# Down projection of a two-layer hybrid backbone: half-precision pairs with one scale a layer in nine of eleven block pairs, and conditioning products 1024 wide

## The chip, the core and the metric

The kernel runs on one core of a Trainium2 chip, as one program in one launch. The metric is the device time of an execution in microseconds (us); the time of a kernel is the median of its runs.

## What is computed

Two transformer-like layers over 1024 latent tokens and 256 context tokens of width 1024. The mixers (Fourier and Hyena in layer 0, neighbourhood attention in layer 1) are not touched. Each layer ends with a gated feed-forward block whose inner width is 2816, scaled and shifted by columns that come from a conditioning vector:

```
def ada_mod(cond, w, b):
    m = (jax.nn.silu(cond) @ w + b)[..., None, :]
    return jnp.split(m, 6, axis=-1)

def swiglu(u, w_gate, w_up, w_down):
    return (jax.nn.silu(u @ w_gate) * (u @ w_up)) @ w_down
...
        h_lat = h_lat + g2 * swiglu(modulate(rms_norm(h_lat, norm2_g[i]), sh2, sc2),
                                    ffn_w_gate[i], ffn_w_up[i], ffn_w_down[i])
```

Everything is float32 in and out. The kernel reaches that precision by splitting an operand x into a high part and the rest, `hi` and `lo`, and adding three products: hi*hi, hi*lo, lo*hi.

## The kernel before, in words

Tokens lie along the free dimension, channels on the 128 partitions. The inner width of 2816 is 22 blocks of 128, taken as 11 pairs of blocks (`n2 = 11`).

**Gate and up** (`ffn`, L1374; one iteration i a pair). Each of gate and up is one Winograd form of a 2x2 block product: seven products in place of eight, each of 12 matmuls (four blocks of the contraction, three hi/lo combinations) of 128x512. `wino_steps` (L1324) gives the matmuls; ScalarE copies partial sums out of PSUM (`snap`, L1329), VectorE adds others (L1338, L1348, L1353). TensorE alternates between the two chains, so that a copy has about one product of the other chain to finish in. Weights and activations here are half-precision (f16) pairs: `half_split` (L1146 on ScalarE, L1147 on VectorE) multiplies by a scale, writes the f16 `hi`, and then `lo`. The scale comes from a bound for each weight tile: `weight_scale` sums absolute values on ScalarE (L1183, with the accumulator) and sums these over the partitions with a matmul.

`finish(i)` multiplies up by the silu of gate (L1422), forms the four hidden blocks' Winograd combinations (L1425 to L1428) and writes seven of them to DRAM (`bops`) on POOL's queue (L274). `sums(i)` does the same for four weight blocks of down (loads on SP's queue, L268; L1388 to L1391; `sops` in DRAM). Layer 0 calls `sums` once an iteration, layer 1 twice in iterations 1 to 5.

**Down** (`down`, L1493). Again a Winograd form over the whole layer: seven products p, each summed over the 11 pairs i, with 12 matmuls a pair (L1511). `operands` loads a weight block and a hidden block, 512 columns each, into one 128x1024 tile, and `split` (L287 on ScalarE, L289 on VectorE) writes fp32r `hi` and `lo` tiles; in four of the seven products the loaded tile is also the `lo` tile. At the end of a product VectorE evicts four PSUM banks into the residual (`evict`, L1532), scaled by a conditioning column. Two sets of four banks alternate. In layer 0 the conditioning products of layer 1 run beside gate, up and Down: `ada_group` multiplies a 128x1024 weight tile by the broadcast conditioning vector and sums along the row, in two halves of 512 (L448) that a third operation adds (L450).

**What sets the order.** The order of instructions on each engine is made at build time, by a scheduler that runs down the program text; each engine then works through its own list. Tiles come from pools in rotation: a tile is free when the last use of the one that had its place is over. The pool `p4` has 20 buffers of 128x1024 float32 (`S4`); Down's operands and the conditioning weights come from it. `T()` takes small tiles from a pool of six and, two times of eight, from another.

## Time and profile before

| | us |
|---|---|
| median of 3 runs (3014.61 to 3021.31) | 3015.26 |
| the profiled execution | 3016.71 |
| its span, first to last instruction | 3014.9 |
| TensorE (PE) busy | 2864.5 |
| VectorE (DVE) busy | 2108.4 |
| ScalarE (ACT) busy | 1511.8 |
| first and last matmul of Down, both layers | 1359.5 and 2996.7 |

Each group row names line, engine, operation, tiles written and read, shapes and count; behind the bar stand the busy time of the group in us (of overlapping instructions only once), the mean duration of one in ns, and the engine's idle time just ahead of them with what ended it. PEld is TensorE's weight load, which runs beside the matmuls. A row of a stretch gives the busy time of each engine in it, with the number of instructions that lie in it wholly or partly, the granted clock, the share of time that the DMA engines were busy, and GB/s. A row of waits gives who waited for whom: total us, times, longest. In a timeline row the time in brackets is the idle time ahead of the instruction and what ended it.

### The profile page before, as it was taken

The numbers are of one execution on the slowest core, as the hardware profiler recorded it, in microseconds if no ns is written. First come the engines' busy times: TensorE is split into PE (matmuls) and PEld (weight loads), VectorE is DVE, ScalarE is ACT, GpSimd is POOL, SyncE is SP. The second block draws the span as 40 slices with busy tenths as digits, with TensorE's granted clock in tenths as the row PEclk, the third lists the DMA queues.
The fourth block names the chain that finished last, engine by engine and source line by source line (L and its number), as shares of the span: only waits on it lengthen the run. The fifth ranks groups of instructions, "written<-read, shape, count | busy, mean of one in ns | idle before, by whom it ended". The sixth has DMA issues, their size and how long they took to land. (4 is left out here: it accounts for less than half of the span.)

```text
span 3014.9 us, 46087 instructions
## 1 busy us (share of the span) xinstructions
PE 2864.5 (95%) x16364; PEld 2085.2 (69%) x16364; DVE 2108.4 (70%) x4181; ACT 1511.8 (50%) x2761; POOL 530.8 (18%) x883
## 2 busy tenths in 40 slices
PE   7899999899998999999999999999999799999997
PEld 3678888888897444447778888878777344444886
DVE  5767786674677988866767437777776898765555
ACT  4663325452456555443445336777774655543433
POOL 1012013451111212131020002222231022112000
PEclk9899999999999999999999999999999899999999
DMA  7564545366555555657874344444555376424663
GB/s 256 190 202 166 176 143 173 119 189 213 200 210 196 211 187 206 221 207 270 290 245 153 126 130 119 134 137 121 180 175 192 134 275 235 149 81 165 217 192 130
DMA packets 253681, 551.47 MB, mean 183 GB/s; under 512 B 33926, under 2 KB 69448, under 8 KB 253450
## 3 DMA queue, kind: packets, MB, share of 16 engines
q1 hardware_dynamic: 191658, 357.63, 35.7%
q0 software_dynamic: 59488, 186.70, 17.5%
q10 hardware_dynamic: 2304, 4.20, 0.4%
q8 instruction: 129, 2.11, 0.3%
q14 instruction: 102, 0.84, 0.1%
HBM read 420.20 MB, written 119.80 MB: 179 GB/s over the span
## 5 line engine op out<-in xcount | busy, mean ns | idle before, releaser
L1324 PE MATMUL ps<-s,s 128*128 128x512 f16 x2100 | 477.3, 383 | 16.5 <-DVE s L1221 8.6
L1324 PEld LDWEIGHTS <-s 128*128 128x128 f16 x2640 | 259.1, 98 | 334.5 <-issue 28.4
L283 PE MATMUL ps<-s,wh 128*128 128x256 f32 (+1 forms) x1780 | 393.6, 327 | 1.5 <-ACT wh L287 1.5
L283 PEld LDWEIGHTS ps<-s,wh 128*128 128x128 f32 x1780 | 293.2, 188 | 36.5 <-ACT wh L287 3.1
L283 PE MATMUL pq<-s,wh 128*128 128x512 f32 (+1 forms) x972 | 297.4, 385 | 4.7 <-DVE s L2088 2.5
L1511 PE MATMUL ps<-s,s 128*128 128x512 f32 (+1 forms) x1000 | 261.2, 384 | 9.0 <-DVE s L289 8.7
L287 ACT CAST s<-s 128x1024 fp32r<-128x1024 f32 (+2 forms) x188 | 171.7, 942 | 180.0 <-DMA s<-d 146.9
L283 PE MATMUL ps<-s,wl 128*128 128x256 f32 (+1 forms) x890 | 257.7, 327 | 2.3 <-DVE wl L289 2.3
L283 PE MATMUL ps<-s,s 128*128 128x64 f16 (+3 forms) x2663 | 216.1, 233 | 24.0 <-DVE st L1800 9.9
L287 ACT CAST wh<-ws 128x1024 fp32r<-128x1024 f32 (+1 forms) x99 | 100.4, 1014 | 265.5 <-PE ps L283 163.8
L289 DVE TENSOR_TENSOR s<-s,s 128x1024 fp32r<-128x1024 f32 (+2 forms) x166 | 190.8, 1182 | 45.7 <-ACT s L287 44.8
L1511 PEld LDWEIGHTS ps<-s,s 128*128 128x128 f32 x1000 | 183.8, 188 | 50.3 <-DVE s L289 14.1
L289 DVE TENSOR_TENSOR wl<-ws,wh 128x1024 fp32r<-128x1024 f32 (+1 forms) x99 | 116.6, 1178 | 128.3 <-ACT wh L287 123.7
L283 PEld LDWEIGHTS pq<-s,wh 128*128 128x128 f32 x972 | 176.3, 191 | 39.4 <-DVE s L2088 2.7
L1324 PE MATMUL ps<-s,wh 128*128 128x512 f16 x624 | 190.9, 386 | 3.1 <-ACT wh L1146 2.1
L283 PE MATMUL ps<-s,mat 128*128 128x512 f32 x684 | 177.2, 405 | 6.8 <-DVE s L289 4.0
L283 PE MATMUL pq<-s,wl 128*128 128x512 f32 (+1 forms) x486 | 180.8, 381 | 0.1
L335 ACT CAST mat<-cs 128x1024 fp32r<-128x1024 f16 (+2 forms) x120 | 111.7, 935 | 132.1 <-PE ps L283 38.0
L283 PEld LDWEIGHTS ps<-s,wl 128*128 128x128 f32 x890 | 163.2, 188 | 20.3 <-DVE wl L289 3.7
L274 POOL DMA_DIRECT2D d<-s x153 | 82.7, 541 | 521.3 <-DVE s L1388 224.3
L283 PEld LDWEIGHTS ps<-s,mat 128*128 128x128 f32 x684 | 130.6, 194 | 42.0 <-DVE s L289 6.8
L1511 PE MATMUL ps<-s 128*128 128x512 f32 (+1 forms) x500 | 152.4, 387 | 1.1 <-ACT s L287 1.0
(393 smaller groups left out, 5825.4 us busy)
## 6 DMA issues: line engine op xcount, KB each, us to landing
s<-d SPq DMA_DIRECT2D x286, 256.0 KB, 3.7
s<-in_down SPq DMA_DIRECT2D x154, 256.0 KB, 4.6
d<-s POOLq DMA_DIRECT2D x137, 256.0 KB, 2.5
d<-tk POOLq DMA_DIRECT2D x98, 256.0 KB, 3.3
s<-in_ada_w POOLq DMA_DIRECT2D x48, 512.0 KB, 4.4
g<-in_bias POOLq DMA_DIRECT2D x128, 192.0 KB, 3.2
s<-in_up SPq DMA_DIRECT2D x46, 512.0 KB, 3.5
s<-in_gate SPq DMA_DIRECT2D x44, 512.0 KB, 4.1
```

The lines of the kernel that those rows point to most:

```text
L274: self.last_ldr = self.nc.gpsimd.dma_start(out, in_).ins
L283: self.nc.tensor.matmul(o, l, r, start=st, stop=sp)
L287: self.last_hi = nc.scalar.copy(hi, src).ins
L289: self.last_lo = eng.tensor_tensor(lo, src, hi.bitcast(F32), SUB).ins
L335: self.nc.scalar.copy(m, st)
L1324: nc.tensor.matmul(ps, x[:, sl], y, start=first and j == 0 and x is wh and y is xh, stop=j == 3 and x is wl, skip_group_check=True)
L1511: m = nc.tensor.matmul(acc[j][:, c0:c1], x[:, sl], y[:, xs], start=first and k == 0, stop=last and k == 2, skip_group_check=True)
```

## The change

Down's operands become f16 pairs in the pairs i = 0 to 8 of each product; pairs 9 and 10 stay fp32r, with both scales multiplied into their weight half. For that, one scale for the weights and one for the hidden blocks is made a layer: absolute sums of each pair's four weight blocks (in `sums`) and four hidden blocks (in `finish`) go to the columns of one tile, `sums_of`; one reduction, one matmul of 18 columns and a few operations on columns (`down_scales`, called in the last iteration of gate and up) give both scales, and the eviction's column takes their inverse. The loaded tile is now always one of its own, and both halves of a pair lie in one tile. The conditioning products of layer 1 are one operation of 1024 elements each. The diff, without its smallest pieces:

```
-    def weight_scale(self, tiles):
...
+    def abs_sums(self, tiles, st):
+
         junk = self.T(BF16, 1024)
         for k, t in enumerate(tiles):
-            nc.scalar.activation(junk[:, :t.shape[1]], t, AF.Abs, scale=2.0 ** -15, accum_out=st[:, k:k + 1])
+            self.nc.scalar.activation(junk[:, :t.shape[1]], t, AF.Abs, scale=2.0 ** -15, accum_out=st[:, k:k + 1])
+
+    def over_partitions(self, sums):
+
+        st = self.pt.tile([P, 16], F32, tag="st", name=self.nm("st"))
+        n = sums.shape[1]
+        sb = st.bitcast(BF16)[:, :n]
+        with self.nc.allow_low_precision(reason="a bound, within a factor of two"):
+            self.nc.vector.tensor_reduce(sb, sums, axis=AX, op=ADD)
         ps = self.PS()
-        self.mm(ps[:, 0:1], self.ones.bitcast(BF16)[:, 1::2], sb[:, 0:1], True, True)
+        self.mm(ps[:, :n], self.ones.bitcast(BF16)[:, 1::2], sb, True, True)
+        return ps[:, :n]
...
             for c in reversed(conds):
+                col = self.ada[(l, c)][:, nb:nb + 1]
+                if where != "s2":
+                    o = t if c == 0 else self.T(BF16, 1024)
+                    nc.vector.tensor_tensor_reduce(o, t, self.condw[c], 1.0, 0.0, MUL, ADD, col)
+                    continue
...
+            if i < nh:
+                self.abs_sums(t, sums_of[:, 4 * i:4 * i + 4])
             nc.vector.tensor_tensor(a22, a21, a22, ADD)
...
                 nc.vector.scalar_tensor_tensor(g, up[k], inv, g, op0=MUL, op1=MUL)
+            if i < nh:
+                self.abs_sums(list(gate.values()), sums_of[:, 4 * (nh + i):4 * (nh + i) + 4])
...
             up.to(1)
+            if i == n2 - 1:
+                scales = self.down_scales(l, nh)
...
+    def down_scales(self, l, n):
+
+        nc = self.nc
+        dc = self.C(8)
+        big, sw, sh, both, inv = dc[:, 0:2], dc[:, 2:3], dc[:, 3:4], dc[:, 4:5], dc[:, 5:6]
+        bounds = self.over_partitions(self.sums_of.rearrange("p (i k) -> p i k", k=4))
+        nc.vector.tensor_reduce(big[:, 0:1], bounds[:, :n], axis=AX, op=MAX)
+        nc.vector.tensor_reduce(big[:, 1:2], bounds[:, n:], axis=AX, op=MAX)
+        nc.vector.tensor_scalar(big, big, 1e-30, None, op0=MAX)
+        nc.vector.reciprocal(dc[:, 2:4], big)
+        nc.vector.tensor_tensor(both, sw, sh, MUL)
+        nc.vector.tensor_tensor(inv, big[:, 0:1], big[:, 1:2], MUL)
+        gcol = self.C(8)
+        nc.vector.tensor_scalar(gcol, self.ada[(l, 0)][:, 40:48], inv, None, op0=MUL)
+        return sw, sh, both, gcol
...
-        def operands(asrc, bsrc, own):
-            hi, lo = self.S4(F32R), self.S4(F32R)
-            f = self.S4() if own else lo.bitcast(F32)
+        def operands(asrc, bsrc, last):
+            f = self.S4()
             self.ld(f[:, :512], asrc)
             self.ld(f[:, 512:], bsrc)
-            self.split(f, hi, lo)
+            fa, fb = f[:, :512], f[:, 512:]
+            if last:
+                hi, lo = self.S4(F32R), self.S4(F32R)
+                nc.scalar.activation(hi[:, :512], fa, AF.Copy, scale=both)
+                nc.scalar.copy(hi[:, 512:], fb)
+                nc.vector.scalar_tensor_tensor(lo[:, :512], fa, both, hi[:, :512].bitcast(F32), op0=MUL, op1=SUB)
+                nc.vector.tensor_tensor(lo[:, 512:], fb, hi[:, 512:].bitcast(F32), SUB)
+            else:
+                t = self.S4(F16, 2048)
+                hi, lo = t[:, :1024], t[:, 1024:]
+                self.half_split(fa, sw, hi[:, :512], lo[:, :512])
+                self.half_split(fb, sh, hi[:, 512:], lo[:, 512:])
             return hi, lo
...
-            nc.vector.scalar_tensor_tensor(t, acc[j][:, c0:c0 + n], self.ada_col(l, pc, 5, nb), t, op0=MUL, op1=ADD)
+            nc.vector.scalar_tensor_tensor(t, acc[j][:, c0:c0 + n], gcol[:, nb:nb + 1], t, op0=MUL, op1=ADD)
...
-                ops = operands(src, bops[i][bk], ak in raw)
+                ops = operands(src, bops[i][bk], i >= n2 - 2)
```

Lines move: in the change L1153 and L1154 are `half_split`, L1187 the absolute sums, L1347 the copies out of PSUM, L1356 an addition to one, L1444 the multiplication in `finish`, L1501 and L1503 the silu, L1585 the eviction in Down, L450 the conditioning product, L1342 the matmuls of gate and up and L1564 those of Down.

ScalarE's list in layer 0, around the start of the fourth pair's up product, reads as follows in before (`g` are gate's hidden blocks and `tk` those of up, `ps` PSUM banks, `ws` and `s4` the next weights):

```order
L1475 ACTIVATE g_2686_10968<-g_2686_10968,c_5_93 128x512
L1146 ACTIVATE wh_2768_11460<-ws_2738_11249,c_5_93 128x1024
L1329 COPY g_2726_11180<-ps_2725_11167 128x512
L1475 ACTIVATE g_2726_11180<-g_2726_11180,c_5_93 128x512
L1329 COPY tk_2748_11332<-ps_2747_11319 128x512
L1183 ACTIVATE t_2800_11588,st_2799_11587<-ws_2797_11583 128x1024
L1183 ACTIVATE t_2800_11588,st_2799_11587<-s4_2798_11584 128x1024
L1329 COPY g_2745_11302<-ps_2725_11167 128x512
```

The same place in the change:

```order
L1153 ACTIVATE wh_2762_11449<-ws_2736_11246,c_5_93 128x1024
L1501 ACTIVATE g_2687_10968<-g_2687_10968,c_5_93 128x512
L1187 ACTIVATE t_2724_11203,c_7_94<-g_2687_10968 128x512
L1187 ACTIVATE t_2724_11203,c_7_94<-g_2688_10982 128x512
L1347 COPY tk_2747_11330<-ps_2746_11317 128x512
L1187 ACTIVATE t_2724_11203,c_7_94<-g_2691_11028 128x512
L1347 COPY g_2723_11172<-ps_2722_11159 128x512
L1501 ACTIVATE g_2723_11172<-g_2723_11172,c_5_93 128x512
L1187 ACTIVATE t_2781_11535,c_7_94<-g_2723_11172 128x512
```

Four sums (L1187) have come between the silu and the copies; the first of them reads a block that VectorE's multiplication (L1444) writes after the silu just ahead of it.

VectorE's list in Down of layer 0, at the end of the second product, in before (`s4` are operands, L1532 the four evictions of that product, L474 sums of squares):

```order
L289 TENSOR_TENSOR s4_3266_14299<-s4_3267_14300,s4_3265_14298 128x1024
L448 ISA s4_3263_14292,ah_3264_14294<-s4_3263_14292,s4_2525_10140 128x512
L448 ISA ah_3264_14294 128x1
L1532 SCALAR_TENSOR_TENSOR s2_3190_13935<-ps_3162_13798,c_13_100,s2_3190_13935 128x512
L1532 SCALAR_TENSOR_TENSOR s2_3191_13937<-ps_3163_13799,c_13_100,s2_3191_13937 128x512
L450 TENSOR_TENSOR c_17_102<-ah_3264_14294 128x1
L1532 SCALAR_TENSOR_TENSOR s2_3192_13939<-pq_3164_13800,c_13_100,s2_3192_13939 128x512
L1532 SCALAR_TENSOR_TENSOR s2_3193_13941<-pq_3165_13801,c_13_100,s2_3193_13941 128x512
L289 TENSOR_TENSOR s4_3273_14337<-s4_3273_14337,s4_3272_14336 128x1024
```

The same place in the change:

```order
L1154 SCALAR_TENSOR_TENSOR s4_3256_14481<-s4_3255_14478,c_3139_13645,s4_3256_14481 128x512 x2
L1154 SCALAR_TENSOR_TENSOR s4_3259_14504<-s4_3258_14501,c_3139_13645,s4_3259_14504 128x512 x2
L1585 SCALAR_TENSOR_TENSOR s2_3175_13928<-ps_3156_13794,c_3143_13656,s2_3175_13928 128x512
L450 ISA s4_3257_14498,c_19_103<-s4_3257_14498,s4_2527_10141 128x1024
L450 ISA c_19_103 128x1
L1585 SCALAR_TENSOR_TENSOR s2_3176_13930<-ps_3157_13795,c_3143_13656,s2_3176_13930 128x512
L1585 SCALAR_TENSOR_TENSOR s2_3177_13932<-pq_3158_13796,c_3143_13656,s2_3177_13932 128x512
L1585 SCALAR_TENSOR_TENSOR s2_3178_13934<-pq_3159_13797,c_3143_13656,s2_3178_13934 128x512
L1550 SCALAR_TENSOR_TENSOR s4_3262_14525<-s4_3260_14521,c_3139_13645,s4_3261_14524 128x512
```

Counted from the start of Down, 22 pairs are split ahead of this eviction in before, which is all of the two products, and 31 in the change, nine pairs into the third. At the ends of the first and the third to sixth products the counts are 14, 33, 44, 55 and 66 in before (the products hold 11, 33, 44, 55 and 66 pairs), and 19, 41.5, 53, 65 and 74 in the change. In layer 1 before is at most one pair ahead from the second product on.

TensorE's list: in the change the matmul of 18 columns of layer 0 stands five whole products of gate and up ahead of the first matmul of Down, which in both kernels is followed by more products of gate and up.

More of the change, by code (lines that the diff above doesn't have):

```diff
@@ L1174, in operand_scale @@
         self.usi = us[:, 1:2]
+    def abs_sums(self, tiles, st):
+        junk = self.T(BF16, 1024)
+        for k, t in enumerate(tiles):
+            self.nc.scalar.activation(junk[:, :t.shape[1]], t, AF.Abs, scale=2.0 ** -15, accum_out=st[:, k:k + 1])
[5 more added lines that the diff above has]
+            self.nc.vector.tensor_reduce(sb, sums, axis=AX, op=ADD)
+        ps = self.PS()
+        self.mm(ps[:, :n], self.ones.bitcast(BF16)[:, 1::2], sb, True, True)
+        return ps[:, :n]
     def weight_scale(self, tiles):
         nc = self.nc
+        st = self.pt.tile([P, 16], F32, tag="st", name=self.nm("st"))
         n = len(tiles)
[L1180 to L1188 removed]
+        self.abs_sums(tiles, st)
+        ps = self.over_partitions(st[:, :n].rearrange("p (i k) -> p i k", i=1))
         k = 3 * len(self.wsc)
         s, b, inv = (self.wcol[:, k + j:k + j + 1] for j in range(3))
[L1191 removed]
+        nc.vector.tensor_scalar(b, ps, 1e-30, None, op0=MAX)
         nc.vector.reciprocal(s, b)
@@ L1487, in ffn, with down @@
         finish(n2 - 1, prev[1])
-        self.down(l, bops, sops, hidc, hs, h, todo, after, keep)
-    def down(self, l, bops, sops, hidc, hs, h, todo, after, keep):
+        self.down(l, scales, bops, sops, hidc, hs, h, todo, after, keep)
+    def down_scales(self, l, n):
[12 more added lines that the diff above has]
+        return sw, sh, both, gcol
+    def down(self, l, scales, bops, sops, hidc, hs, h, todo, after, keep):
         nc, a = self.nc, self.a
```

19 lines of the change are left out of this document (8 added, 11 removed).

## The prediction

> **What bounds the kernel now.** I read the page's head first, then busy time by stretch, then TensorE's rate and its waits in the stretches that the change touches. "FFN" below is gate and up with their Winograd products, "Down" the stage that the change rewrites, 0 and 1 the layer.
>
> ```profile
> PE 2864.5 (95%) x16364; PEld 2085.2 (69%) x16364; DVE 2108.4 (70%) x4181; ACT 1511.8 (50%) x2761; POOL 530.8 (18%) x883
> ```
>
> TensorE is busy 95% of the span, so the time falls only where its matmuls come closer together or where it stops waiting. The next rows are stretches of FFN 0, Down 0, the dense start of FFN 1, and Down 1: length, then busy time (count) of each engine, granted clock, DMA share, GB/s.
>
> ```profile
> 1040.00:1360.00 320.00, 316.85 (x1473) 143.52 (x1472) 257.91 (x522) 155.90 (x246) 70.02 (x130) 0.99 0.58 205
> 1376.00:1596.00 220.00, 210.90 (x923) 170.44 (x922) 155.17 (x271) 91.94 (x115) 33.28 (x63) 1.00 0.77 268
> 2400.00:2500.00 100.00, 98.34 (x460) 44.25 (x458) 89.39 (x156) 59.04 (x97) 21.58 (x40) 1.00 0.68 248
> 2765.00:2996.00 231.00, 229.99 (x1065) 184.93 (x1064) 125.94 (x141) 92.43 (x109) 8.09 (x15) 1.00 0.56 182
> ```
>
> Both FFNs and Down 1 keep TensorE fed; only Down 0 does not (210.90 of 220). The rate comes from two quiet stretches, counting the instructions of one line: 120 us of the FFN line, on half-precision operands, and 160 us of the Down line, on fp32r operands.
>
> ```profile
> 2600.00:2720.00 120.00, 120.00 (x557) 53.86 (x555) 1.00 0.27 101
> 2800.00:2960.00 160.00, 160.00 (x708) 132.48 (x707) 1.00 0.60 192
> ```
>
> At full clock and with no idle time a half-precision matmul of 512 columns takes 120/557 = 215.4 ns, an fp32r one 160/708 = 226.0 ns. The DMA share differs too (0.27, 0.60), but FFN 0 ran at 0.58 with 316.85/1473 = 215.1 ns, so it isn't the DMA. What differs is the operand, and with it the weight load:
>
> ```profile
> L1324 PEld LDWEIGHTS <-s 128*128 128x128 f16 x2640 | 259.1, 98 | 334.5 <-issue 28.4 <-ACT s L1146 1.1
> L1511 PEld LDWEIGHTS ps<-s,s 128*128 128x128 f32 x1000 | 183.8, 188 | 50.3 <-DVE s L289 14.1
> ```
>
> **Part A: the rate.** Nine pairs of eleven turn half-precision: 9 x 12 matmuls x 7 products = 756 a layer. Each gains 226.0 - 215.4 = 10.6 ns: 8.0 us a layer, **16 us** in both. In Down 1, where TensorE waits 1 us in 231, all of it is on the path. Upper end 16; the lower end, nothing, is the second rival.
>
> The Trainium skill speaks against this part: "TensorE: Matmul & The Clock Gate", section "Back-to-back issue gap", gives the gap of single warm matmuls as columns / 2.4 + 2.5 ns whatever the operand, 216 ns at 512 columns, and its section "Step-by-step: what each phase is for" says that the next weights load while the current matmul runs. By that rule A would be 0. The half-precision row agrees (215.4), the fp32r row (226.0) does not; the measurement decides.
>
> **Part B: the feeding of Down 0.** At 226.0 ns its 923 matmuls would take 208.6 us; the stretch has 220, so 11.4 us are lost. Who was waited for there, by TensorE, then by SP's queue:
>
> ```profile
> PE ps L1511 <- DVE s L289: 7.8, 8, 1.8
> PE ps L1511 <- ACT s L287: 1.0, 1, 1.0
> ...
> SPq L268 <- PE ps L1511: 54.2, 27, 4.6
> ```
>
> TensorE waits 8.8 us for splits (`lo` on VectorE, `hi` on ScalarE), and SP's loads wait for TensorE to give buffers back. The timeline at the end of the second product shows how:
>
> ```profile
> 1433.95 1.41 DVE L1532 SCALAR_TENSOR_TENSOR s<-ps,c,s 128x512 f32<-128x512 f32 x2 [8.00 <-PE ps L1511]
> ...
> 1435.34 1.40 DVE L1532 SCALAR_TENSOR_TENSOR s<-pq,c,s 128x512 f32<-128x512 f32 x2
> ...
> 1436.66 1.22 DVE L289 TENSOR_TENSOR s<-s,s 128x1024 fp32r<-128x1024 f32 x1
> ...
> 1437.93 2.11 PE L1511 MATMUL ps<-s,s 128*128 128x512 f32 x8 [1.75 <-DVE s L289]
> ```
>
> VectorE stands 8 us at the eviction of the product that TensorE is finishing; the split for the next product's first pair stands behind it, so TensorE waits 1.75 us. The order shown above says how many pairs were split ahead of that eviction: 0 in before (22 splits stand ahead of it, all used), 9 in the change (31), since a pair now holds one buffer to its last matmul, and one for the load only until it is split, where it held two to the last matmul. Nine pairs are 9 x 12 x 0.215 = 23 us of matmuls, against 2.8 us for four evictions. So the eight waits should go. I take **8 us** of the 11.4, near the 8.8 that the rows name; the ends are 0 and 11.4.
>
> What is late next there: DMA or VectorE. The same bytes in 220 - 8 - 8 = 204 us need 268 x 220/204 = 289 GB/s, and the first product already ran above that with TensorE fed:
>
> ```profile
> 1376.00:1406.00 30.00, 29.60 (x130) 24.54 (x131) 1.00 0.86 310
> ```
>
> The splits cost more. A 1024-wide cast and subtraction become two 512-wide ones each, with a scale:
>
> ```profile
> L287 ACT CAST s<-s 128x1024 fp32r<-128x1024 f32 (+2 forms) x188 | 171.7, 942 | 180.0 <-DMA s<-d 146.9 <-DVE tk L1353 4.5 <-PE pq L1511 4.4
> L289 DVE TENSOR_TENSOR s<-s,s 128x1024 fp32r<-128x1024 f32 (+2 forms) x166 | 190.8, 1182 | 45.7 <-ACT s L287 44.8 <-PE pq L1324 0.7
> L1146 ACT ACTIVATE s<-t,c 128x512 f16<-128x512 f32 x176 | 116.6, 710 | 17.1 <-DVE c L1192 16.8 <-DVE t L1303 0.3
> L1147 DVE SCALAR_TENSOR_TENSOR s<-t,c,s 128x512 f16<-128x512 f32 x176 | 126.6, 746 | 2.8 <-ACT s L1146 2.8
> ```
>
> A pair costs ScalarE 1.42 us instead of 0.94 and VectorE 1.49 instead of 1.18; 63 pairs a layer add 30 us and 20 us. In Down 0 ScalarE goes to 122 of 204 us, VectorE to 175 of 204 (86%), in Down 1 VectorE to 146 of 223. A pair's matmuls last 12 x 0.215 = 2.58 us, above both: hidden, at 0. If VectorE were the bound in Down 0, B would be lost: the first rival.
>
> **Part C: the bounds in the FFNs.** Each layer gets 72 absolute sums on ScalarE, 512 wide. Before has four of that form, with a read of the accumulator behind each:
>
> ```profile
> L1183 ACT ACTIVATE t<-g x4: 617/628/632, 2313.4 to 2316.2; 128x512 bf16<-128x512 f32 x4
> L1183 ACT ACTIVATION_READ_ACCUMULATOR t<-g x4: 186/187/189, 2313.9 to 2316.8; 128x1 f32 x4
> ```
>
> At 0.63 + 0.19 = 0.82 us a sum they add 59 us of ScalarE a layer. An iteration of FFN has 14 products of 12 matmuls, 14 x 12 x 0.215 = 36 us; eight sums add 6.6 us to it, so FFN 0 goes from 49% to 67%; iterations 1 to 5 of FFN 1 take two sets of down sums each, twelve in all, and go from 59% to 86%. TensorE needs its ScalarE copies within one product (2.6 us). The work itself is hidden, but each engine keeps to its list, so a sum that waits for a landing or for VectorE holds back the copies behind it, and VectorE's last subtraction in `finish`, which overwrites a block that a sum reads, now waits for that sum, with the additions that empty PSUM behind it. What a late copy costs, before shows in FFN 1:
>
> ```profile
> 2507.62 0.59 ACT L1329 COPY g<-ps 128x512 f32<-128x512 f32 x1 [8.85 <-DMA d<-g]
> 2508.26 1.12 PE L1324 MATMUL ps<-s,s 128*128 128x512 f16 x4 [2.75 <-ACT g L1329]
> 2509.10:2512.50 3.40, 3.40 (x9) 1.22 (x8) 2.99 (x6) 3.39 (x5) 0.00 (x0) 0.50 0.18 72
> ```
>
> The copy had to wait (for a buffer that a write to DRAM gave back), TensorE idled 2.75 us and then ran 3.4 us at half clock: 2.75 + 1.7 = 4.5 us an event. VectorE gets lighter on the other side: a conditioning product was two halves and an addition, and is now one.
>
> ```profile
> L448 DVE CUSTOM_DVE_ANT_0 s<-s,s 128x512 f32<-128x512 f32 x160 | 109.7, 700 | 13.0 <-DMA s<-in_ada_w 12.4 <-PE ps L1324 0.5
> L448 DVE DVE_READ_ACCUMULATOR2_ANT ah<- 128x1 f32 x256 | 20.8, 81 | 0.0
> L450 DVE TENSOR_TENSOR c<-ah 128x1 f32<-128x1 f32 x128 | 18.6, 152 | 0.7
> L1147 DVE SCALAR_TENSOR_TENSOR wl<-ws,c,wh 128x1024 f16<-128x1024 f32 x44 | 56.4, 1281 | 18.7 <-ACT wh L1146 18.7
> ```
>
> 2 x (0.70 + 0.08) + 0.15 = 1.71 us goes; the 1024-wide one isn't in the trace and lies between one half (0.78) and, by the last row, 1.28 + 0.08 = 1.36. I take 1.36, nearest in width: 0.35 us less, 64 times, 38 of them in FFN 0. It has no term of its own; it offsets part of C. I take **+4 us** for C, about one event more than now. The ends: -9, if the event above and a like one of FFN 0 go, and +45, an event in every second of some 20 iterations.
>
> **Part D: the bound product.** One matmul of 18 columns and seven VectorE operations on a few columns a layer (0.15 us each by the L450 row, 1.1 us together), then the first split. Five FFN products of 2.6 us stand between that matmul and the first Down matmul in TensorE's order; the chain needs 1.1 + 1.42 + 1.49 = 4 us. I take 0; the other end is one event of 4.5 us a layer.
>
> **Sum.** -16 - 8 + 4 = -20. The profiled execution took 3016.71 us, of which 3014.9 is the span; it becomes 2996.7. The median shown is 3015.26, 1.5 lower: **2995**. About 0.2%, 6 us, can be told from no change here.
>
> **Rivals.**
> 1. Down 0 stays unfed (B = 0): DMA or VectorE takes the place of the evictions. For it: VectorE at 86%, DMA share 0.77. Against it: the stretch at 310 GB/s, and nine pairs of slack. 3015 - 16 + 4 = 3003.
> 2. The matmul rate stays (A = 0), as the page's rule has it, or because the fp32r rate belongs to the stage. Against it: 215.1 ns at the same DMA share. 3015 - 8 + 4 = 3011.
> 3. Slower: ScalarE's fixed order in the FFNs, above all at 86% in iterations 1 to 5 of FFN 1. A sum waits for VectorE's multiplication, a copy stands behind the sum, TensorE stops. At 4.5 us it decides from 24/4.5, six events, on; with ten, 3015 - 24 + 45 = 3036. For it: the event above, and the rows of the order where a sum stands ahead of a copy. Against it: most copies have a whole other product between them and their use.
> 4. The bound comes late (D = 9): 2995 + 9 = 3004, near the first.
>
> **Chances.** Forecast 0.60, with 2984 to 3006 its own range; first and fourth rival 0.22; second 0.07; third 0.11. Faster by over 0.2% (below 3009): 0.82, the forecast and the cases at 3003. Within: 0.08, mostly the second. Slower: 0.10. The range runs from 2984 (A whole, B 11.4, C -4) to 3013, past the second rival, and leaves out the third.
>
> **What would show it.** In the changed profile: the Down line at 215 to 216 ns by count in Down 1, weight loads at 98 ns; Down 0 some 16 us shorter with no wait on splits at product ends; FFN stretches with ScalarE near 67% and 86%, and TensorE's idle time there within a few us of now. I am wrong if the Down line stays at 226 ns, if Down 0's waits go to loads, or if copies behind sums appear among TensorE's waits in the FFNs with half-clock stretches after them.

## The result, and the profile after

Five runs of the changed kernel took 2997.35 us at the median (2994.25 to 3003.99), beside 3015.99 of the kernel before on the same chip (3014.61 to 3021.31): a ratio of 0.9937, 95% interval 0.9918 to 0.9956. The profiled execution took 2994.77 us, of which 2993.0 is the span: 21.9 less than before. The forecast was 2995 us.

The head of the page after: TensorE 20 us less, ScalarE 137 us more.

```profile
PE 2844.3 (95%) x16366; PEld 1951.5 (65%) x16366; DVE 2132.5 (71%) x4159; ACT 1648.9 (55%) x3201; POOL 530.7 (18%) x883
```

The same four stretches as before (FFN 0, Down 0, the dense start of FFN 1, Down 1), shifted to where they lie now: length, busy time (count) of PE, PEld, DVE, ACT and POOL, granted clock, DMA share, GB/s.

```profile
1040.00:1355.00 315.00, 313.22 (x1466) 142.11 (x1465) 258.30 (x458) 195.27 (x361) 72.12 (x134) 1.00 0.62 212
1373.00:1575.00 202.00, 199.87 (x924) 104.43 (x923) 158.67 (x265) 110.71 (x183) 32.86 (x62) 1.00 0.82 280
2376.00:2476.00 100.00, 92.01 (x417) 40.78 (x416) 85.13 (x147) 74.31 (x154) 19.16 (x36) 0.97 0.66 231
2745.00:2975.00 230.00, 230.00 (x1108) 122.00 (x1107) 148.07 (x230) 118.93 (x191) 8.09 (x15) 1.00 0.57 187
```

Down 0's stretch, with 924 matmuls, is 202 us long where it was 220 with 923; VectorE is busy 79% of it, and not the 86% that the forecast feared. The third row is the other side: in 100 us of FFN 1 TensorE idles 8 where it idled 1.7, and the clock is 0.97.

The rate by count, Down's line alone: 160 us of Down 1, then 160 us of Down 0.

```profile
2780.00:2940.00 160.00, 160.00 (x735) 83.03 (x734) 1.00 0.65 212
```
```profile
1385.00:1545.00 160.00, 160.00 (x734) 84.12 (x733) 1.00 0.90 313
```

That is 160/735 = 217.7 ns and 160/734 = 218.0 ns against 226.0 before; nine pairs at 215.4 and two at 226.0 would average 217.3. The weight loads of the half-precision pairs take 98 ns:

```profile
L1564 PEld LDWEIGHTS <-s 128*128 128x128 f16 x1536 | 148.5, 98 | 179.2 <-issue 6.7 <-ACT s L1153 0.8
```

The next rows are TensorE's waits in Down 0, after. Before, they were 8.8 us in nine places, five of them at the first pair of a product. Now they are 2.1 us in two places near 1570 us, at the end of the stage, where the context columns' matmuls begin among Down's:

```profile
PE ps L1564 <- DVE s L1154: 1.7, 1, 1.7
PE ps L1564 <- ACT s L1153: 0.4, 1, 0.4
```

In FFN 1 (2376 to 2765 us) it is the other way round: TensorE waits more than before. Late copies on ScalarE cost it 10.4 us where they cost 2.7:

```profile
PE ps L1342 <- ACT g L1347: 10.4, 3, 5.4
PE ps L1342 <- DVE wl L1154: 2.0, 1, 2.0
```

The next rows show the largest of these on ScalarE's timeline and on TensorE's, and the half-clock stretch that follows:

```profile
2418.26 0.63 ACT L1187 ACTIVATE t<-g 128x512 bf16<-128x512 f32 x1 [3.25 <-DVE g L1444]
...
2425.79 0.59 ACT L1347 COPY g<-ps 128x512 f32<-128x512 f32 x1 [4.12 <-DMA d<-g]
```
```profile
2426.42 1.86 PE L1342 MATMUL ps<-s,s 128*128 128x512 f16 x4 [5.37 <-ACT g L1347]
```
```profile
2424.80:2431.60 6.80, 5.18 (x13) 1.82 (x13) 2.10 (x3) 5.81 (x10) 0.00 (x0) 0.50 0.78 295
```

A sum waits 3.25 us for VectorE's product of gate and up, three more sums follow, then a copy waits 4.12 us for a buffer `g` that a write to DRAM (`d<-g`, POOL's queue) gives back. TensorE idles 5.4 us, and the clock is 0.50 for 6.8 us.

Ahead of FFN 1 TensorE's list has changed too. Its timeline after, in the output projection of attention:

```profile
2278.99 1.87 PE L283 MATMUL pq<-c,tk 128*128 128x1 f32 x8 [3.86 <-DVE tk L481]
2282.74 2.07 PE L283 MATMUL ps<-t,c 128*128 128x512 f32 x2 [1.88 <-ACT t L505]
```

These are the norm's matmuls for the first 512 tokens (`rms_begin`, `rms_end`). Before, they stood 36 matmuls later in TensorE's list, with 30 other matmuls between them, and neither was waited for; now the first comes too early and the second right behind it. The norm of the other 512 tokens has gone the opposite way. Before, its matmuls were waited for; after, the first of them starts at 2333.96 us without a wait, and so does the second:

```profile
2353.11 1.05 PE L283 MATMUL ps<-c,tk 128*128 128x1 f32 x8 [3.05 <-DVE tk L474]
2356.72 2.07 PE L283 MATMUL pq<-t,c 128*128 128x512 f32 x2 [2.55 <-ACT t L498]
```
```profile
2333.96 0.95 PE L283 MATMUL ps<-c,tk 128*128 128x1 f32 x8
```

By the starts of TensorE's matmuls the new order costs nothing in the end: from a matmul of this projection that has the same place in all lists (2274.5 us before, 2251.2 after) to the 121st of FFN 1 it takes 127.6 us before and 128.0 after, and 126.3 to 130.8 in all kernels below, whichever of the two orders they have.

**Stage by stage**, from the starts of TensorE's matmuls in the traces of all kernels below (us; "idle" is TensorE's, in that stage). The first column ends at FFN 0's first matmul; the second at Down 0's last; the third begins at the last matmul of the context columns' down projection and ends at the 301st matmul of FFN 1; the fourth ends at Down 1's last. The fifth overlaps these two: it runs from the 121st matmul of FFN 1 to Down 1's last.

```
kernel                        to FFN 0  FFN 0 + Down 0  to the 301st  rest of FFN 1 + Down 1  from the 121st
before                         966.0   634.6 (idle 14.7)    776.5       553.6 (idle 3.8)      594.7 (idle  5.4)
after                          964.5   612.9 (idle  6.5)    782.7       548.8 (idle 5.3)      596.0 (idle 13.0)
after, again (e7)              968.5   613.3                784.4       548.8 (idle 5.1)      596.8 (idle 13.6)
e1 Down in fp32r               971.8   633.0 (idle 14.5)    784.2       561.1 (idle 8.0)      608.4
e2 hi and lo in two buffers    974.2   615.2 (idle  7.3)    782.7       549.9                 599.6
e3 both tile counters kept     971.1   613.0                781.3       539.3 (idle 0.2)      585.7 (idle  5.1)
e4 sums spread                 975.1   611.5                780.6       539.0 (idle 0.0)      583.3 (idle  4.3)
e5 counters kept and spread    965.6   617.2                776.9       539.5 (idle 0.2)      584.6 (idle  4.4)
e6 counters kept, no sums      967.9   615.9                775.6       540.1                 582.8 (idle  2.6)
e8 wide conditioning only      967.7   633.3                775.5       553.5                 594.6
e9 fp32r, split in halves      970.2   626.0 (idle  9.0)    778.0       559.1                 606.3
e10 two buffers, in place      969.0   616.3 (idle  6.6)    781.2       546.1                 593.2
e11 PSUM counter kept          971.3   611.5                778.5       539.9 (idle 0.1)      586.8 (idle  5.5)
e12 as e5, ten pairs           976.7   612.8                778.9       539.4                 585.7
```

So the change gained 21.7 us in the second column and 4.8 in the fourth, and lost 6.2 in the third. Part A alone is worth 8 in the fourth: something there took gains away. The loss of the third is no loss of the norm's: the 301st matmul of the change is the one that waits 5.4 us for the copy (2426.42 us). The fifth column has these events together, and none of the norm: 1.3 us more than before, where A alone would give 8 less.

### The profile page after: what moved, and what is told of

The parts are those of the page before. It is cut to its first block, busy times and chain, and to the rows that moved or that the text cites. A ratio compares the mean times of both kernels' runs of the same rounds, so it can differ in the third digit from the quotient of the medians.

```text
span 2993.0 us, 46520 instructions
## 1 busy us (share of the span) xinstructions
PE 2844.3 (95%) x16366; PEld 1951.5 (65%) x16366; DVE 2132.5 (71%) x4159; ACT 1648.9 (55%) x3201; POOL 530.7 (18%) x883
## 5 line engine op out<-in xcount | busy, mean ns | idle before, releaser
L1342 PE MATMUL ps<-s,s 128*128 128x512 f16 x2340 | 526.3, 381 | 15.4 <-ACT g L1347 12.8
L1342 PEld LDWEIGHTS <-s 128*128 128x128 f16 x2640 | 258.7, 98 | 338.6 <-issue 32.7
L1564 PE MATMUL ps<-s 128*128 128x512 f16 (+2 forms) x1308 | 302.9, 378 | 2.1 <-DVE s L1154 1.7
L1153 ACT ACTIVATE s<-s,c 128x512 f16<-128x512 f32 x295 | 200.5, 715 | 118.6 <-DMA s<-d 85.7
L1564 PEld LDWEIGHTS <-s 128*128 128x128 f16 x1536 | 148.5, 98 | 179.2 <-issue 6.7
L1154 DVE SCALAR_TENSOR_TENSOR s<-s,c,s 128x512 f16<-128x512 f32 x295 | 210.5, 746 | 65.7 <-ACT s L1153 64.9
L1342 PE MATMUL ps<-s,wh 128*128 128x512 f16 x624 | 189.9, 382 | 3.0 <-ACT wh L1153 1.7
L283 PEld LDWEIGHTS ps<-s,s 128*128 128x128 f32 (+1 forms) x743 | 112.9, 191 | 35.2 <-DVE s L614 4.2
```

The lines of the kernel that those rows point to most:

```text
L283: self.nc.tensor.matmul(o, l, r, start=st, stop=sp)
L1153: nc.scalar.activation(hi, src, AF.Copy, scale=scale)
L1154: nc.vector.scalar_tensor_tensor(lo, src, scale, hi, op0=MUL, op1=SUB)
L1342: nc.tensor.matmul(ps, x[:, sl], y, start=first and j == 0 and x is wh and y is xh, stop=j == 3 and x is wl, skip_group_check=True)
L1564: m = nc.tensor.matmul(acc[j][:, c0:c1], x[:, sl], y[:, xs], start=first and k == 0, stop=last and k == 2, skip_group_check=True)
```

## The experiments

The theories as forecast: A is the operand's own rate, B comes from how far the splits run ahead, which the buffers set, C are events behind the sums. Rival to B: what feeds Down 0 is something else in the split. Rival to C: the lost time comes from the order that the scheduler makes, and not from the sums. Each ratio is to the kernel before, run beside it on the same chip.

**e7, the change again.** No edit.

> The changed kernel once more, beside the other runs, to see what of its stage times repeats. Theory: the waits at its places repeat (1.7 and 0.4 us for splits at the end of Down 0, 5.8 us for the norm's column ahead of FFN 1, 10 to 11 us for ScalarE's copies in FFN 1 in three or four places), since each engine's list is fixed; 2994 to 3002 us. Rival, that they shift by some us with the start of the transfers: other places, and the total within the same bounds.

2999.81 us, ratio 0.9936 (0.9911 to 0.996). The third and fourth columns repeat (784.4, 548.8), and the waits with them: 11.4 us in four places for copies `g`, and 5.8 us for what the expectation calls the norm's column. (That one is the bound of a weight tile of gate or up, L1195, for which VectorE waits 5.1 us for ScalarE's sum of the tile.) The losses belong to the program, not to one execution. What doesn't repeat is the first column, the same matmuls in all these kernels: 964.5 to 976.7 us, so differences of some us between totals say little, and stages are compared.

**e1, Down back in fp32r.**

```
-                t = self.S4(F16, 2048)
-                hi, lo = t[:, :1024], t[:, 1024:]
-                self.half_split(fa, sw, hi[:, :512], lo[:, :512])
...
+            hi, lo = self.S4(F32R), self.S4(F32R)
+            f = self.S4() if last else lo.bitcast(F32)
...
+            self.split(f, hi, lo)
```

> The change with Down's operands back as fp32r pairs in the buffers of before (so a 1024-wide cast and subtraction again, no scale); the absolute sums, the bound product and the wide conditioning products stay. By the forecast's parts A and B, both Downs get their old rate of 226.0 ns a matmul (756 x 10.6 ns = 8 us a layer) and Down 0 gets its 8 to 10 us of waits for splits back: 2995 + 16 + 9 = 3020 us, with Down 0 some 18 us longer than in the change and Down 1 some 8 us. Rival, that the rate or the feeding came from something else in the change (fewer VectorE operations, other order): one of the two stays at its new length, 3003 to 3011 us.

3036.1 us, ratio 1.0065 (1.005 to 1.008): slower than before, by more than the forecast of A and B. Against the repeated change, FFN 0 and Down 0 take 19.7 us more and the fourth column 12.3 more (8 for the rate, and splits are waited for in Down 1 too). The waits of Down 0 are back:

```profile
PE ps L1554 <- DVE s L289: 7.5, 8, 1.8
PE ps L1554 <- ACT s L287: 2.9, 2, 2.1
```

A and B together are real, and the rest of the change by itself loses about 19 us, 15 of them in the third and fourth columns. It does not yet say what B is.

**e2, hi and lo in two buffers; e10, the same in exactly the buffers of before; e9, fp32r with each split cut in two.** The three edits:

```
-                t = self.S4(F16, 2048)
-                hi, lo = t[:, :1024], t[:, 1024:]
+                hi, lo = self.S4(F16, 2048)[:, :1024], self.S4(F16, 2048)[:, :1024]
```
```
+                hi = self.S4(F16, 2048)[:, :1024]
+                lo = f.bitcast(F16)
...
+                self.half_split(fb, sh, hi[:, 512:], lo[:, 1024:1536])
```
```
-            self.split(f, hi, lo)
+            for q in (slice(0, 512), slice(512, 1024)):
+                nc.scalar.copy(hi[:, q], f[:, q])
+                nc.vector.tensor_tensor(lo[:, q], f[:, q], hi[:, q].bitcast(F32), SUB)
```

> The change, but a half-precision pair takes two buffers, one for hi and one for lo, and holds both to its last matmul, as an fp32r pair did before. Operands, operations and their widths stay. In VectorE's order 4, 3.5, 2, 1.5, 1 and 0 pairs are then split ahead of the evictions of Down 0's products 1 to 6, against 8 to 10 in the change; in Down 1 5 to 6 against 11 to 12. By part B (the buffers set how far the splits run ahead, and that decides who is waited for), the products 4 to 6, with under 2 pairs ahead, wait again for splits, 1 to 2 us each: Down 0 4 to 8 us longer than in the change, 2999 to 3003 us, the Down line still at 215 to 216 ns by count, Down 1 unchanged. Rival, that Down 0 is fed because the evictions or VectorE got lighter, not because of the buffers: no wait on splits, 2995 us.

> The change with half-precision pairs in exactly the buffers of before: hi in one, lo written over the loaded data in the other, both held from the load, or the split, to the pair's last matmul. 5 to 7 pairs stand split ahead of the evictions of Down 0 in VectorE's order. Theory of the split's width: FFN 0 and Down 0 stay at 613 to 615 us and the waits at products' ends stay away, 2997 to 3001 us. Rival, part B as forecast (two held buffers a pair let loads and splits fall back): 619 to 623 us, with waits for splits at most ends, 3004 to 3009 us.

> The kernel with Down's operands as fp32r pairs in the buffers of before, but each pair's cast and subtraction cut into two of 512 columns, the width that the half-precision splits have. In VectorE's order 5 to 7 pairs are then split ahead of the evictions of Down 0, with the same two buffers a pair, where the 1024-wide splits had 0. Theory, that the width of the split, through the order that follows from it, feeds Down 0, and neither the buffers nor the operand: no waits at the ends of products, so FFN 0 and Down 0 together 613 + 8 (the rate) = 621 to 623 us, 11 us less than with whole fp32r splits (633.0), Down 1 at 226 ns; 3018 to 3024 us. Rival, part B as forecast, that a pair holding two buffers is what starves it: 631 to 633 us, 3030 to 3036 us in all.

Measured: e2 3006.16 us, ratio 0.9962 (0.9948 to 0.9977); e10 2998.17, 0.994 (0.992 to 0.9961); e9 3018.9, 1.0011 (1.0 to 1.0023). What the three say stands in one table. "Ahead" counts the pairs in VectorE's list that are split ahead of the first eviction of products 1 to 6 of Down 0, beyond those already used; "waits" are TensorE's for splits in Down 0.

```
kernel   operand, width of a split   buffers a pair holds           ahead            waits
before   fp32r, 1024                 2 from the load on             3, then 0        8.8 us, 9
e1       fp32r, 1024                 2                              2, then 0        10.4 us, 10
e2       f16, 512                    1 to the split, then 2 more    4 3.5 2 1.5 1 0  3.7 us, 5
e9       fp32r, 512                  as before                      5 to 7           2.6 us, 3
e10      f16, 512                    2                              5 to 7           2.2 us, 2
after    f16, 512                    1 to the split, then 1 more    8 to 10          2.1 us, 2
```

(In e1, e9 and before, three of the seven products hold a third buffer until the split.) In e2 TensorE waits after the evictions of product 5 (from 1522.8 us) and product 6 (from 1553.0), with 1 pair and none ahead, and inside product 7. Behind products 1 to 4, with 1.5 pairs and more, it doesn't:

```profile
1530.73 1.02 PE L1563 MATMUL ps<-s,s 128*128 128x512 f16 x4 [0.54 <-DVE s L1154]
1533.93 1.02 PE L1563 MATMUL ps<-s,s 128*128 128x512 f16 x4 [0.45 <-DVE s L1154]
1556.46 1.89 PE L1563 MATMUL ps<-s,s 128*128 128x512 f16 x8 [1.24 <-DVE s L1154]
1575.14 1.02 PE L1563 MATMUL ps<-s,s 128*128 128x512 f16 x4 [1.32 <-DVE s L1154]
```

FFN 0 and Down 0 of e2 are 1.9 us longer than in the repeated change, and not the 4 to 8 expected; e2's total is 3 us above its range, which these stages don't explain. e10's 616.3 us are 1.3 above its theory, with 10.3 us at half clock by the trace's clock records where the repeated change has 4.5.

So the splits that run ahead are what feeds Down 0, as part B had it. But the single buffer is not needed for it: e10 has the buffers of before and no wait at a product's end, and e9 has fp32r operands in those buffers and none either; its 2.6 us all lie after 1577 us, at the end of the stage. What before lacked was the narrow split: in the two versions with 1024-wide ones (before, e1) the next pairs' splits stand behind the evictions in VectorE's list from the second product on. Why the scheduler places them there was not tried. e9 misses its 621 to 623 us by 3: the fp32r rate is that of before, in Down 0 too:

```profile
1400.00:1560.00 160.00, 160.00 (x708) 132.53 (x707) 1.00 0.88 308
```

and of the 13 us to the repeated change the rate is 8, the idle time 3. The total is in its range. e9 also says what part A is: 226.0 ns at a DMA share of 0.88 here and of 0.60 in before's Down 1, 218.0 ns at 0.90 in the change; the operand sets it, not the stage.

**e3, both tile counters kept; e11, the PSUM counter alone.** Tiles are dealt from two pools in turn by a counter (`T`), PSUM tiles by another (`PS`). The sums' outputs and the bound product advance them, so everything later gets other tiles. e3 leaves both where they were (`count` is true for the sums of the weight tiles alone, which before has too), e11 only the second, by the first of these edits:

```
+        pk = self.pk
         bounds = self.over_partitions(self.sums_of.rearrange("p (i k) -> p i k", k=4))
+        self.pk = pk
```
```
-        junk = self.T(BF16, 1024)
+        if count:
+            junk = self.T(BF16, 1024)
+        else:
+            junk = self.pt.tile([P, 1024], BF16, tag="t", name=self.nm("t"))
...
                     o = t if c == 0 else self.T(BF16, 1024)
+                    if c:
+                        self.tk = (self.tk + 1) % 8
```

> The change, but its new tiles (the outputs of the absolute sums, the bound product's PSUM tile, the wide conditioning product's one output where there were two) don't move on the two counters that deal out later tiles between pools, so that what follows Down 0 gets the pools it had before. No work is changed. Between the end of attention and FFN 1's first matmul the change lost 7 us of what it had gained by then (-22.7 to -15.9). Theory: that is the order of TensorE's list there (the norm's matmul stands 36 matmuls earlier than before, its second right behind it), which follows from the dealt tiles; here the old order is back, so the 7 us return: 2988 us, with the step from the values to FFN 1 at -22 again. Rival, that the 7 us come from another phase between the engines after a shorter Down 0, or differ from run to run: 2995 us and the same step.

> The change, but only the counter of PSUM tiles stays as it was at the bound product; the outputs of the sums and of the conditioning products still move the other counter. TensorE's list ahead of FFN 1 is then that of before. Theory: the PSUM counter alone sets that order and the copy waits of FFN 1 come from the same order, since which products lie in which pool follows from it: the stage from 300 matmuls into FFN 1 to the end of Down 1 at 539 us as with both counters kept, against 548.8 in the change, and 2992 to 2995 us. Rival, that the pool of the sums' outputs makes the copies late: the 548.8 stay, 2998 to 3001 us.

e3 2992.89 us, ratio 0.9925 (0.9908 to 0.9941); e11 2989.35, 0.9911 (0.9894 to 0.9928). In both the norm's matmuls are back at their old places in TensorE's list: those of the first 512 tokens aren't waited for, those of the others are again, 6.3 us in e3 for 5.6 before. So e3's theory fails: the 7 us that the old order was to bring back had been made up in the change by the 121st matmul of FFN 1, and from the projection to there e3 takes 128.6 us where the change took 128.0 and 128.6. The third column gains 1.4 and 4.2 us against the first execution of the change, 3.1 and 5.9 against the second; a new wait at 2420 us (below) stands in it. What gains is FFN 1: 9 us in the fourth column and 9 to 11 in the fifth, which e3's expectation didn't have and e11's did. The copies of FFN 1 aren't late any more, and TensorE doesn't stop. The change, then e11, each from some us after the 301st matmul:

```profile
2426.00:2756.00 330.00, 324.31 (x1497) 146.17 (x1497) 237.10 (x411) 204.97 (x386) 61.90 (x115) 0.99 0.48 172
```
```profile
2432.00:2760.00 328.00, 327.90 (x1535) 148.71 (x1534) 237.43 (x412) 201.49 (x379) 61.89 (x115) 1.00 0.47 171
```

ScalarE has the same work in both, twelve sums an iteration included. So the twelve sums alone don't make the copies late; it takes the order as well, and one PSUM tile a layer, taken by the bound product, is enough to change that. (Which of the places that moved does it was not tried.)

**e4, the sums of layer 1 spread.**

```
-            for k in (2 * i - 2, 2 * i - 1) if l == 1 else (9, 10) if i == 9 else (i,) if i < 9 else ():
+            for k in (9, 10) if i == 9 else (i,) if i < 9 else ():
```

> The change, but layer 1 reads and sums one down block pair an iteration over all of FFN 1, as layer 0 does, instead of two an iteration in iterations 1 to 5: ScalarE then has 8 sums an iteration instead of 12. Theory (part C): the 12 us that FFN 1 and the waits there lose (TensorE waits 10.4 us for late ScalarE copies in three places, plus half-clock stretches) come from the doubled sums in the first iterations; they go or shrink to one event: 2985 to 2990 us, no copy wait over 2 us in FFN 1, half-clock 0 to 3 us. Rival, that one sum's place in ScalarE's list matters and not how many there are: the same waits at other places, 2993 to 2998 us.

2994.54 us, ratio 0.9921 (0.9907 to 0.9936): the total lies in the rival's range. With the order ahead of FFN 1 as in the change, the fourth column falls to 539.0 us, TensorE idle 0.0:

```profile
2436.00:2765.00 329.00, 329.00 (x1541) 149.31 (x1540) 244.55 (x424) 211.54 (x397) 62.19 (x115) 1.00 0.51 181
```

Here the total hides 9 us of gain: the profiled execution's first column is 975.1, against 964.5 and 968.5. The rival (the same waits at other places) falls: in the fifth column TensorE idles 4.3 us, and 13 in the change. Yet ScalarE's sums still wait for VectorE as they did in the change, 34.5 us against 35.9. What went is the wait of copies for the write: 19.0 us in six places, then 2.9 in five.

```profile
ACT t L1187 <- DVE g L1444: 35.9, 13, 7.8
ACT g L1347 <- DMA d<-g: 19.0, 6, 7.2
```
```profile
ACT t L1187 <- DVE g L1444: 34.5, 12, 9.3
...
ACT g L1347 <- DMA d<-g: 2.9, 5, 1.2
```

In this stage a sum that waits costs TensorE nothing; a copy whose buffer is still being written out does. Either edit, another order or one down pair at a time, brings the buffers back in time. The second edit moves more than absolute sums: the loads of the down blocks, VectorE's additions to them and their writes to DRAM on POOL's queue, all in `sums(i)`, are spread as well. Which link of that chain (the sums, VectorE's list, POOL's queue) is the late one was not isolated.

**e5, both edits together; e6, the counters kept and no sums.** e5 is e3 and e4. e6 is e3 with

```
+        nc.vector.memset(self.sums_of, 0.0625)
...
-            if i < nh:
-                self.abs_sums(t, sums_of[:, 4 * i:4 * i + 4])
...
-            if i < nh:
-                self.abs_sums(list(gate.values()), sums_of[:, 4 * (nh + i):4 * (nh + i) + 4])
```

> Both edits together: later tiles dealt as before, and layer 1's down blocks read and summed one pair an iteration. If the two losses are two places with a cause each (the order of TensorE's list ahead of FFN 1; the doubled sums in FFN 1's first iterations), both are gone: from the end of Down 0 to FFN 1's first matmul 2 to 3 us less than before as with the first edit alone, and from there to the end no ScalarE copy, split or sum that TensorE waits over 2 us for after the first product, as with the second alone: 2980 to 2986 us. Rival, that a loss only moves to another place when one is taken away (the first edit alone had FFN 1's event at a split instead of a copy): 2990 to 2995 us.

> The kernel with later tiles dealt as before, without the absolute sums of down blocks and gate blocks: the bound product reads constants that are written once, so the bounds don't follow the data. This leaves out 72 sums a layer and nothing else. Theory, that the sums cost one event in FFN 1 (there, with the sums, ScalarE stands 4.1 us at a sum of a gate block that VectorE hasn't multiplied yet; TensorE idles 3.5 and 1.4 us for the splits behind it and runs 6.8 us at half clock): 8 to 9 us less than with them, 2983 to 2986 us, and FFN 0 within 2 us. Rival, that the sums are hidden and the event is the first iterations' own (loads, VectorE): within 2 us of 2993.

e5 2986.69 us, ratio 0.9893 (0.9874 to 0.9912); e6 2988.53, 0.99 (0.9878 to 0.9922). e6's price of the sums is smaller than expected: 5.7 us less than e3 in the third column, 2.9 in the fifth. Most of that is the wait at 2420 us. In e3 a sum waits for VectorE there and a split of gate's first row stands behind it on ScalarE:

```profile
2423.17 0.63 ACT L1192 ACTIVATE t<-g 128x512 bf16<-128x512 f32 x1 [4.13 <-DVE g L1449]
...
2424.55 1.13 ACT L1155 ACTIVATE wh<-ws,c 128x1024 f16<-128x1024 f32 x1
```
```profile
2425.74 1.03 PE L1347 MATMUL pq<-s,wh 128*128 128x512 f16 x2 [3.53 <-ACT wh L1155]
2428.18 0.61 PE L1347 MATMUL pq<-s,wl 128*128 128x512 f16 x1 [1.41 <-DVE wl L1156]
```

Without sums, the same split is done at 2420.6 us and TensorE doesn't wait for it. In e5, with the spread sums, the third column is 776.9 us, within a few tenths of before (776.5), and the fourth 539.5. The copies are in time, but the place of 2420 us is still there, with waits of 2.4 and 1.8 us in place of 3.5 and 1.4; by the fifth column e5 is 1.8 us above e6, which has no sums. Its total is 0.7 us above its range, less than its executions differ (2981.10 to 2990.87).

**e8, the wide conditioning products alone,** on the kernel before.

> The kernel before with only the 1024-wide conditioning products: no sums, no bound, fp32r pairs in both Downs. By the forecast they have no term of their own: VectorE loses 64 x 0.35 = 22 us of work, 13 of them in FFN 0, where it is hidden; 3013 to 3016 us, beside 3016. Rival, that VectorE's lighter list in FFN 0 and at the start of FFN 1 is what shortened these stages: FFN 0 3 to 4 us shorter as in the change, 3010 us.

3017.85 us, ratio 0.9997 (0.9985 to 1.0009): no term, as costed, though 2 us above the range. The second column is 1.3 us under before, so the rival's 3 to 4 us don't show. In the trace of the change the 1024-wide product takes 1.22 us, and its accumulator 0.08: 1.30 in place of the 1.36 that I took:

```profile
L450 DVE CUSTOM_DVE_ANT_0 s<-s,s 128x1024 f32<-128x1024 f32 x48 | 58.4, 1216 | 3.3 <-DMA s<-in_ada_w 3.3
```

**e12, e5 with ten pairs in half precision.** (`sums_of` has 80 columns for it.)

```
-        nh = n2 - 2
+        nh = n2 - 1
...
-                ops = operands(src, bops[i][bk], i >= n2 - 2)
+                ops = operands(src, bops[i][bk], i >= n2 - 1)
```

> Later tiles dealt as before and layer 1's down blocks summed one pair an iteration, and ten pairs of eleven in half precision instead of nine: 2 x 84 matmuls gain 10.6 ns, 1.8 us in all, for eight more sums a layer: 2983 to 2986 us beside 2986.7 of the same with nine pairs. Rival, that the bound is late now, since the tenth pair's gate blocks are multiplied and summed just ahead of the bound product: one wait of TensorE of 3 to 5 us a layer at the first split, 2988 to 2995 us.

2990.82 us (2981.83 to 2995.28), ratio 0.9909 (0.9891 to 0.9927), beside 0.9893 for nine pairs: the intervals overlap, and 1.8 us can't be told here. Its third column is 2.0 us longer than e5's, its fourth the same; TensorE waits for nothing where layer 0's bound is made (1340 to 1390 us), and for nothing at the start of Down 1, so the rival's late bound doesn't show. Whether the tenth pair gains its 1.8 us stays open. e5 has the lowest median of these kernels, 30 us below the kernel before; e11, one counter put back, is 26 below.

## Why the prediction was right, and where its steps failed

**The total is right, and partly by luck.** The forecast was -16 for A, -8 for B and +4 for C, -20 in all. The stages of the profiled execution give -15.4, -10.4 and +5.5, and -1.6 in stages that no part is about: -21.9. Each term is near its forecast, but the stretch ahead of FFN 0 alone differs by 12 us between executions of these kernels, so that the totals agree within 2 us is luck. Two of the reasons failed as well.

**A holds as it was worked out.** 226.0 to 217.7 ns over 924 matmuls is 7.7 us a layer, against 8.0. e9 brings the 226.0 back, in both layers. By the formula of the Trainium skill for the isolated matmul ("TensorE: Matmul & The Clock Gate", section "Back-to-back issue gap"), which has no term for the operand, A would have been 0: the measurement agrees with it for the half-precision operands alone (215.4 ns).

**B has about the right size and half the reason.** From FFN 0's last matmul to Down 0's last it took 224.2 us before and 206.1 after. Of these 18.1 us the rate is 7.7; the other 10.4 are B, for the 8 forecast and 11.4 at most. The waits that the trace names there fell by 6.7 us, its idle time by 7.0; the last 3 us it assigns to nothing. (FFN 0 has the other 3.6 of the second column's 21.7: 1.3 idle time, and 2.1 of half clock, 7.1 to 2.8 us by the clock records.) The failed step is "since a pair now holds one buffer to its last matmul": with two buffers (e10) and even with fp32r operands (e9) the ends are fed. The splits ahead of the eviction decide, as I said, and with the buffers of before the width of a split decided whether there were any (e1, e9). Buffers come second: 8 to 10 pairs ahead with one, 5 to 7 with two in place, 4 to 0 with three.

**C is near its size by two larger things that cancel.** FFN 1 and Down 1 lost 9.1 us beside A's gain, 6.2 in the third column and 7.7 - 4.8 = 2.9 in the fourth: two events and not the one forecast. FFN 0's 3.6 us make it +5.5. Inside it, the sums, with the order that came with them, cost 13 us (fifth column, 596.0 against 582.8 in e6, which leaves out these sums and keeps the counters). But e6 lacks the event of before at 2507 us as well, some 5 us, and so do e3, e4, e5 and e11: with A that makes their fourth column 14 us shorter than before, 8 for the rate, 3.6 idle, 1.7 half clock. Why that event went was not tried.

The mechanism that I named exists: a sum waits for VectorE, what stands behind it on ScalarE is late, half clock follows (e3's 2420 us). A sign that the prediction named for being wrong also came in the change: copies behind sums among TensorE's waits, half clock behind the largest, and 13.0 us idle in the fifth column for 5.4. Yet these copies wait for buffers and not for the sum ahead of them, and how long they do hangs on the order too: with the same sums, keeping the PSUM counter (e11) takes 9 of the 13 us away, and spreading the down pairs (e4) nearly all. The failed step is that the forecast took the lists as fixed and added sums to them; the sums and the bound product also move the tile counters, and so change lists in stages that no edit touches. The rows of the order on which the prediction rested lie around the edits; the norm's place, where the list changed as well, lies 700 us behind Down 0, though that change cost nothing.

**D was 0,** as forecast: TensorE waits for nothing between 1340 and 1373 us, where the bound of layer 0 is made. ScalarE's shares were forecast at 67% in FFN 0 and 86% in the dense start of FFN 1; they are 62% and 74%.

**The rivals.** The first (Down 0 unfed) and the second (the rate stays) are refuted by the rows above. The third, slower by events in the FFNs, decided from six events on; FFN 1 has four, three copies and a split (12.4 us).

## What to carry to other kernels

Where a scheduler makes the lists and counters deal out tiles, an added tile can move instructions far behind the edit: compare the order of the whole program, not only around the change, and take new scratch tiles from pools or counters of their own. When an order has changed, follow the time to a later matmul that all orders share before a wait is called a loss: the norm's two new waits were made up 100 us later. An engine that must evict and prepare operands keeps TensorE fed only as far as preparation stands ahead of the eviction in its list; cutting a preparation in two can be enough to get it there, before any buffer is added. When a total agrees with a forecast, check the stages: here a cost of 13 us and an event of some 5 that went stood inside a term forecast at 4.

## What the runs showed of the hardware that I had not expected

The stretch ahead of FFN 0, with the same matmuls in all kernels, took 964.5 to 976.7 us, and most of the difference is the granted clock: the two ends have 38 and 58 us at half clock by the trace's clock records, which is 10 us of work. The mean clock of 0.98 and 0.97 in the rows is all that a page shows of it:

```profile
0.00:964.40 964.40, 909.88 (x5165) 762.09 (x5166) 668.64 (x1380) 449.49 (x717) 187.65 (x247) 0.98 0.56 188
```
```profile
0.00:976.60 976.60, 916.60 (x5165) 766.80 (x5166) 668.11 (x1380) 449.10 (x717) 187.10 (x247) 0.97 0.56 185
```

That alone is half of what the change was worth.
